# Moving TensorE's transposes and attention products one to three k tiles later in its order

## The chip, the cores and the metric

The kernel runs on one core of a Trainium2 chip. The metric is the device time of one execution in microseconds (us); lower is better. Three runs of the kernel before took 2409.83, 2411.72 and 2412.51 us (median 2411.72). For this kernel a difference of about 0.2% (4.8 us) is what can be told from no change.

## The reference

Two transformer-like blocks in float32 over 256 tokens of width 2048. The first block mixes a gated causal convolution with a causal attention that adds a forgetting bias, then a square-ReLU feed-forward of width 8192. The second block has attention with a relative-position bias, a multi-window pooling branch, and a gated feed-forward of width 5632 whose up-projection passes a three-tap causal convolution. Cut to what the change touches:

```
q, k = heads; p = softmax(q @ k.T * scale + bias); a = p @ v          # both blocks, 8 heads
u = rmsnorm(x) @ w_up                                                  # 2048 -> 2 * 5632
y = conv_b + conv_w[0]*u[t-2] + conv_w[1]*u[t-1] + conv_w[2]*u[t]
gate, val = split(y);  x = x + (silu(gate) * val) @ w_down
```

## The kernel before

Every large product is cut into chunks of up to 512 output columns (`add_chunk`). A chunk reads weight tiles of 512 rows; a weight tile is four k tiles of 128 rows, and two k tiles make a unit. Each weight is split on chip into a high part `wh` (a cast on ScalarE, L846) and a remainder `wl` (a subtraction on VectorE, L847); the activations are split likewise into two halves of a `k_...` tile (`split_out`, L155 to L166). One k tile costs TensorE six matmuls (`both`, L887): high by high, low by high and high by low, for two token blocks. At the start of a unit the split of the unit three places ahead is issued (L901), and `wh` and `wl` have four buffers each, so ScalarE and VectorE run at most a few units ahead of TensorE.

TensorE's program order is written out by the kernel itself. The main loop (L898) issues a k tile, adds one to `now`, and then `run_due` takes up to three of the tasks from a heap whose due time has come. `later(delay, fn)` puts a task `delay` k tiles ahead, `chain` puts a row of steps at one k tile each, and `need(key)` runs tasks ahead of their due time until a named operand has been issued. The queues themselves run in the order of issue, so a task due at k tile 2 stands on TensorE behind two k tiles of the next chunk, and what comes after it waits with it.

At the end of a chunk its evacuation is issued: on ScalarE for the scaled chunks (`evac_scaled`, L440), on VectorE for the residual sum (`evac_add`, L543). The result must then be turned so that tokens lie along the free dimension. `turned` does that on VectorE in 16 small pieces; `transposed` does it on TensorE, as two tasks (b = 0 and 1) of four 128x128 transposes each (L175), `gap` k tiles apart, and chains the steps of its user behind each.

- In the up-projection of the second block, chunks alternate: a gate chunk "g" (turned on VectorE, then convolution L479 and L484, sigmoid L745, product L746) and a value chunk "v" (transposed on TensorE, then convolution, product with the gate L740, and the split into `k_d`, L155 and L162). There are 11 pairs, in groups of 4, 4 and 3; each group is followed by its down-projection, whose k tiles read `k_d` in the order of the pairs. The variable `soon` marks the very last v chunk (j = 10).
- When a chunk of the residual is finished, `to_acts` makes the next layer's activations from it. For the last of four (n == 3) TensorE transposes `xs[3]`; this happens for the layers named "f", "i" and "g" (and "h" at the start). `squares` (L227) and the norm's factor (`rstd_of`) follow at once; for "i" the tasks `final_norm` rescale `xs` later (L582).
- `head_task` issues the eight heads of either attention as seven tasks: scores, biased, exps, normal, turn (three transposes of the probabilities, L351), keep (a copy on ScalarE, L355) and values (L360, L361). Heads are 6 k tiles apart in the first block and 7 in the second. The second attention's last head feeds the output projection, which asks for it by `need("2a1 3")`.

Of the kernel before, what the change touches and what calls it, by code (L numbers as in the profile page):

```python
# [61 lines left out]
def tile_two_blocks(  # L62
# [30 lines left out]
    def later(delay, fn, *keys):  # L93
        seq[0] += 1
        heapq.heappush(tasks, (now[0] + delay, seq[0], fn, keys))

    def chain(delay, stages, *keys, gap=1):

        for i, fn in enumerate(stages):
            later(delay + i * gap, fn, *(keys if i == len(stages) - 1 else ()))  # L100
# [11 lines left out]
    def need(*keys):  # L112
        for key in keys:
            while key not in ready:
                run_one()


    xs = [const.tile([P, TB, CW], F32, name=f"x{n}") for n in range(4)]
# [28 lines left out]
    def split_out(key, j, n, p, scales=None):  # L147

        if key not in K:
            kt_tile(key)  # L150
        hi, lo = (K[key][:, h, j:j + n, :] for h in range(2))

        def to_hi():
            if scales is None:
                S.copy(hi, p)  # L155
            else:
                for i in range(n):
                    S.activation(hi[:, i, :], p[:, i, :], AF.Copy, scale=scales[i])

        def to_lo():  # L160
            if scales is None:
                V.tensor_tensor(out=lo, in0=p, in1=hi.bitcast(F32), op=OP.subtract)  # L162
            else:
                for i in range(n):
                    V.scalar_tensor_tensor(out=lo[:, i, :], in0=p[:, i, :], scalar=scales[i],
                                           in1=hi[:, i, :].bitcast(F32), op0=OP.mult, op1=OP.subtract)  # L166
        return [to_hi, to_lo]

    def transposed(z, use, delay, keys=(), gap=1, lag=1, step=1):

        def task(b, mine):
            p = tr_p.tile([P, 2, T], F32, tag="tr", name="p_t")
            for j in range(2):
                for tb in range(TB):
                    TE.transpose(p[:, j, tb * P:(tb + 1) * P], z[:, tb, (2 * b + j) * P:(2 * b + j + 1) * P], ident)  # L175
            chain(lag, use(b, p), *mine, gap=step)
        for b in range(2):
            later(delay + gap * b, lambda b=b: task(b, keys[2 * b:2 * b + 2]))
# [22 lines left out]
    def group_keys(key):  # L201
        return [f"{key} {j}" for j in range(4)]
# [38 lines left out]
    def to_acts(name, n, gcol, delay):  # L241

        key = f"{name}{n}"
        def use(b, p):
            return split_out(key, 2 * b, 2, p, [gcol[:, 4 * n + 2 * b + i:4 * n + 2 * b + i + 1] for i in range(2)])
        if name == "h" or n == 3:
            transposed(xs[n], use, delay, group_keys(key), lag=0, step=0)
        else:
            turned(xs[n], use, delay, group_keys(key), rate=2, lag=3)

# [54 lines left out]
    def head_task(blk, h, delay):  # L305

        half, hh = divmod(h, 4)
        cols = (slice(0, P), slice(P, MAXCOL))
        t = {}

        def scores():
            need(f"{blk}q{half} {hh}", f"{blk}k{half} {hh}")
            qk = AT[blk, "qk", half]
            p = t["p"] = tr_p.tile([P, 512], F32, tag="tr", name="p_s")
            TE.matmul(p[:, 0:P], qk[:, 0, hh, 0:P], qk[:, 1, hh, 0:P], start=True, stop=True)
            TE.matmul(p[:, P:3 * P], qk[:, 0, hh, P:T], qk[:, 1, hh, :], start=True, stop=True)  # L316

        def biased():
            if blk == 1:
                need(f"1nb{half}")  # L320
            nb, p = AT[blk, "nb", half], t["p"]
            s = t["s"] = s_p.tile([P, CW], F32, tag="s", name="s_att")[:, 0:MAXCOL]
            st = t["st"] = st_p.tile([P, 6], F32, tag="sm", name="sm")
            if blk == 1:
                for i in range(2):
                    V.scalar_tensor_tensor(out=s[:, cols[i]], in0=p[:, cols[i]], scalar=AT["c"][:, i, h:h + 1],
                                           in1=nb[:, hh, cols[i]], op0=OP.add, op1=OP.add)
            else:
                need(f"rq{half}")
                for i in range(2):  # L330
                    V.scalar_tensor_tensor(out=s[:, cols[i]], in0=p[:, cols[i]],
                                           scalar=AT["rq", half][:, 4 * i + hh:4 * i + hh + 1],
                                           in1=nb[:, hh, cols[i]], op0=OP.mult, op1=OP.add)
            for i in range(2):
                V.tensor_reduce(st[:, i:i + 1], s[:, cols[i]], AX.X, OP.max, negate=True)

        def exps():
            s, st = t["s"], t["st"]
            for i in range(2):
                S.activation(s[:, cols[i]], s[:, cols[i]], AF.Exp, bias=st[:, i:i + 1], accum_out=st[:, 2 + i:3 + i])  # L340

        def normal():
            s, st = t["s"], t["st"]
            V.reciprocal(st[:, 4:6], st[:, 2:4])
            for i in range(2):
                V.tensor_scalar(s[:, cols[i]], s[:, cols[i]], st[:, 4 + i:5 + i], None, op0=OP.mult)

        def turn():
            p = t["p"] = tr_p.tile([P, 512], F32, tag="tr", name="p_p")
            for i in range(3):  # L350
                TE.transpose(p[:, i * P:(i + 1) * P], t["s"][:, i * P:(i + 1) * P], ident)  # L351

        def keep():
            t["pt"] = pt_p.tile([P, MAXCOL], F32, tag="pt", name="pt")
            S.copy(t["pt"], t["p"][:, 0:MAXCOL])  # L355

        def values():
            v, pt = AT[blk, "v"], t["pt"]
            p = tr_p.tile([P, 2, T], F32, tag="tr", name="p_t")
            TE.matmul(p[:, 0, :], v[:, 0, h * P:(h + 1) * P], pt[:, 0:T], start=True, stop=False)  # L360
            TE.matmul(p[:, 0, P:T], v[:, 1, h * P:(h + 1) * P], pt[:, T:MAXCOL], start=False, stop=True)  # L361
            chain(1, split_out(f"{blk}a{half}", hh, 1, p[:, 0:1, :]), f"{blk}a{half} {hh}")
        for i, fn in zip((0, 1, 2, 3, 6, 7, 8), (scores, biased, exps, normal, turn, keep, values)):
            later(delay + i, fn)

    def qk_use(blk, half, which, scale=None):
# [108 lines left out]
    def conv3(o, u, w, bias):  # L475

        def last():
            for i in range(2):
                S.activation(o[:, i, :], u[:, i, :], AF.Identity, bias=bias(i), scale=w(i, 2))  # L479

        def before():
            for i in range(2):
                for d in (1, 2):
                    V.scalar_tensor_tensor(out=o[:, i, d:T], in0=u[:, i, 0:T - d], scalar=w(i, 2 - d), in1=o[:, i, d:T],  # L484
                                           op0=OP.mult, op1=OP.add)
        return [last, before]
# [242 lines left out]
    def evac_up(which, j, key):  # L729
        def then(z):  # L730
            cv = z_p.tile([P, 4, T], F32, tag="z", name="z_cv")

            def use(b, p):
                a = cv[:, 2 * b:2 * b + 2, :]
                c0 = (0 if which == "g" else 44) + 4 * j + 2 * b
                steps = conv3(a, p, lambda i, t: ccol[:, t, c0 + i:c0 + i + 1], lambda i: ccol[:, 3, c0 + i:c0 + i + 1])
                if which == "v":
                    g = FU["g", j][:, 2 * b:2 * b + 2, :]
                    need(f"gate{j} {2 * b}")
                    return steps + [lambda: V.tensor_tensor(out=a, in0=a, in1=g, op=OP.mult), *split_out(key, 2 * b, 2, a)]  # L740
                t = {}

                def sigmoid():
                    t["s"] = s_p.tile([P, 2, T], F32, tag="s", name="sg")
                    S.activation(t["s"], a, AF.Sigmoid)  # L745
                return steps + [sigmoid, lambda: V.tensor_tensor(out=a, in0=a, in1=t["s"], op=OP.mult)]  # L746
            if which == "g":
                FU["g", j] = cv
            if which == "g":
                turned(z, use, 2, group_keys(f"gate{j}"), rate=2)  # L750
            else:
                soon = j == FF2 // CW - 1
                transposed(z, use, 1 if soon else 2, group_keys(key), gap=1 if soon else 2)
        return then


# [204 lines left out]
```

## Time and profile before

| | us |
|---|---|
| median of three runs | 2411.72 |
| the profiled execution, own time | 2411.87 |
| its span, first to last instruction | 2410.1 |
| VectorE busy | 1662.6 (69%) |
| ScalarE busy | 1158.9 (48%) |

The profile is of one execution. "Idle before, releaser" in a row says how long the engine stood idle just before the instruction and what ended that. A busy matmul row is not a matmul at its peak, since matmuls are pipelined. The granted clock is 1.00 in nearly all of the 40 slices of the page; the mean of the execution is 0.995. Weights come by 1 MB transfers, 445.8 MB in all, at 189 GB/s over the span.

### The profile page before, as it was taken

Reading aid. Unit: us, or ns where it says so; the run is one execution under the profiler, and the core shown is the slowest. Engines: PE = TensorE matmul, PEld = TensorE weight load, DVE = VectorE, ACT = ScalarE, POOL = GpSimd, SP = SyncE. Lnnn points to the kernel's source line nnn. Section 1 sums busy time; section 2 is a strip of 40 time slices with the busy share of each in tenths; the row PEclk is TensorE's granted clock in tenths of the full one; section 3 lists DMA queues with packets and bytes.
Section 4 is the critical chain, followed back from the end, with each engine's and each line's share of the span. In section 5 each row is a group of like instructions: output and inputs, shape, how many; then the busy total and the mean of one; then the engine's idle time right before and its main releaser. Section 6 shows DMA issues by size and latency. Waiting matters only on the chain.

```text
span 2410.1 us, 27828 instructions
## 1 busy us (share of the span) xinstructions
PE 2369.9 (98%) x10649; PEld 1962.8 (81%) x10649; DVE 1662.6 (69%) x2293; ACT 1158.9 (48%) x1514; POOL 36.5 (2%) x53
## 2 busy tenths in 40 slices
PE   9899999999999999999999999999999999999999
PEld 9688888888888888888888887888778888888877
DVE  5487776666877567577477856667787467865884
ACT  5355444444454354354345446545555345544453
POOL 1000000000000000000000000000000000000000
PEclk9899999999999999999999999999999999999999
DMA  7755565655556556555555665555555555555554
GB/s 256 188 183 171 197 207 194 210 202 176 192 179 206 192 190 195 192 192 192 192 186 181 197 209 194 161 177 190 180 181 193 192 185 182 188 194 185 185 175 140
DMA packets 230966, 456.67 MB, mean 189 GB/s; under 512 B 8085, under 2 KB 15997, under 8 KB 230832
## 3 DMA queue, kind: packets, MB, share of 16 engines
q1 hardware_dynamic: 227584, 445.81, 56.4%
q0 software_dynamic: 3248, 9.08, 1.6%
q8 instruction: 83, 1.36, 0.2%
q14 instruction: 51, 0.42, 0.0%
HBM read 451.18 MB, written 3.67 MB: 189 GB/s over the span
## 4 chain that ended last, share of the span: by engine, by line
PE 88%; DVE 6%; ACT 3%; DMA 2%; issue 1%; SPq 0%; ACTq 0%
PE acc L887 85%; DVE wl L847 2%; DVE z_t L190 2%; ACT wh L846 2%; DMA raw<-in_w_in_dram 2%; DVE z_cv L484 1%; PE p_t L175 1%; ACT z L440 1%; PE acc_last L887 0%; ACT z_cv L479 0%; PE p_t L360 0%; PE p_s L316 0%; PE p_t L714 0%; PE p_p L351 0%; DVE x L543 0%
## 5 line engine op out<-in xcount | busy, mean ns | idle before, releaser
L847 DVE TENSOR_TENSOR wl<-raw,wh 128x1024 fp32r<-128x1024 f32 (+1 forms) x848 | 1022.1, 1214 | 653.1 <-ACT wh L846 565.2
L846 ACT CAST wh<-raw 128x1024 fp32r<-128x1024 f32 (+1 forms) x848 | 874.9, 1042 | 726.3 <-PE acc L887 671.0
L887 PE MATMUL acc<-wh,k_g 128*128 128x512 f32 x1408 | 379.3, 391 | 0.0
L887 PE MATMUL acc<-wh,k_h 128*128 128x512 f32 (+1 forms) x1344 | 352.5, 384 | 12.7 <-ACT wh L846 12.7
L887 PEld LDWEIGHTS acc<-wh,k_g 128*128 128x128 f32 x1408 | 263.6, 188 | 53.9
L887 PEld LDWEIGHTS acc<-wh,k_h 128*128 128x128 f32 x1344 | 248.5, 189 | 58.5 <-ACT wh L846 14.0
L887 PE MATMUL acc<-wh,k_u 128*128 128x512 f32 x1024 | 274.8, 389 | 4.5 <-DVE k_u L162 4.5
L887 PE MATMUL acc<-wh,k_f 128*128 128x512 f32 x1024 | 273.9, 389 | 0.0
L887 PEld LDWEIGHTS acc<-wh,k_u 128*128 128x128 f32 x1024 | 191.9, 188 | 45.8 <-DVE k_u L162 6.2
L887 PEld LDWEIGHTS acc<-wh,k_f 128*128 128x128 f32 x1024 | 192.1, 188 | 39.7
L887 PE MATMUL acc<-wl,k_g 128*128 128x512 f32 x704 | 217.5, 390 | 0.0
L887 PE MATMUL acc<-wl,k_h 128*128 128x512 f32 (+1 forms) x672 | 201.4, 381 | 0.0
L887 PE MATMUL acc<-wh,k_d 128*128 128x512 f32 x656 | 176.9, 392 | 0.0
L887 PE MATMUL acc<-wl,k_f 128*128 128x512 f32 x512 | 157.6, 389 | 0.0
L887 PE MATMUL acc<-wl,k_u 128*128 128x512 f32 x512 | 157.6, 389 | 0.0
L887 PEld LDWEIGHTS acc<-wl,k_g 128*128 128x128 f32 x704 | 132.6, 188 | 27.9
L190 DVE STREAM_TRANSPOSE z_t<-z 32x256 f32<-32x256 f32 x336 | 146.4, 436 | 5.6
L887 PEld LDWEIGHTS acc<-wl,k_h 128*128 128x128 f32 x672 | 125.4, 189 | 23.2 <-DVE wl L847 0.3
L887 PEld LDWEIGHTS acc<-wh,k_d 128*128 128x128 f32 x656 | 123.2, 189 | 25.2
L887 PE MATMUL acc<-wh,k_i 128*128 128x512 f32 x512 | 140.0, 395 | 0.0
L190 DVE STREAM_TRANSPOSE z_t<-z_f 32x256 f32<-32x256 f32 x256 | 111.5, 436 | 4.1
L887 PEld LDWEIGHTS acc<-wl,k_f 128*128 128x128 f32 x512 | 96.1, 188 | 20.0
(227 smaller groups left out, 2010.3 us busy)
## 6 DMA issues: line engine op xcount, KB each, us to landing
raw<-in_w_ff_dram SPq DMA_DIRECT2D x128, 1024.0 KB, 5.2
raw<-in_w_in_dram SPq DMA_DIRECT2D x104, 1024.0 KB, 5.1
raw<-in_w_up_dram SPq DMA_DIRECT2D x88, 1024.0 KB, 5.0
raw<-in_w_down_dram SPq DMA_DIRECT2D x44, 1024.0 KB, 5.1
raw<-in_w_mix_out_dram SPq DMA_DIRECT2D x16, 1024.0 KB, 5.1
raw<-in_w_out_dram SPq DMA_DIRECT2D x16, 1024.0 KB, 5.1
raw<-in_w_conv_out_dram SPq DMA_DIRECT2D x8, 1024.0 KB, 5.3
raw<-in_w_attn_out_dram SPq DMA_DIRECT2D x8, 1024.0 KB, 5.5
```

The lines of the kernel that those rows point to most:

```text
L175: TE.transpose(p[:, j, tb * P:(tb + 1) * P], z[:, tb, (2 * b + j) * P:(2 * b + j + 1) * P], ident)
L190: V.transpose(dst, src)
L440: S.activation(z[:, tb, :], acc[:, tb, :], AF.Copy, scale=R[rname][:, tb:tb + 1])
L484: V.scalar_tensor_tensor(out=o[:, i, d:T], in0=u[:, i, 0:T - d], scalar=w(i, 2 - d), in1=o[:, i, d:T], op0=OP.mult, op1=OP.add)
L846: S.copy(wh[:, :, 0:ncol], raw)
L847: V.tensor_tensor(out=wl[:, :, 0:ncol], in0=raw, in1=wh[:, :, 0:ncol].bitcast(F32), op=OP.subtract)
L887: TE.matmul(halves[tb][:, 0:ncol], k[:, i, kt, tb * P:(tb + 1) * P], w[:, kk, 0:ncol], start=begin and first and kt == 0, stop=end and stop)
```

## The change

Three places get other due times; no instruction is added or removed.

- `to_acts`: the transposes of the last residual chunk of the layers "f", "i" and "g" are due 5 and 6 k tiles after the evacuation instead of 2 and 3 ("h" is as it was).
- `head_task`: turn is due 7 k tiles after the head's start instead of 6, keep 8 instead of 7, values 10 instead of 8; the two split steps behind values move with it, from 9 and 10 to 11 and 12.
- `evac_up`, v chunks: the transposes are due at 3 and 5 instead of 2 and 4, and for the very last v chunk at 2 and 3 instead of 1 and 2; the five steps chained behind each move with them.

```diff
@@ to_acts
-            transposed(xs[n], use, delay, group_keys(key), lag=0, step=0)
+            transposed(xs[n], use, delay if name == "h" else delay + 3, group_keys(key), lag=0, step=0)
@@ head_task
-        for i, fn in zip((0, 1, 2, 3, 6, 7, 8), (scores, biased, exps, normal, turn, keep, values)):
+        for i, fn in zip((0, 1, 2, 3, 7, 8, 10), (scores, biased, exps, normal, turn, keep, values)):
@@ evac_up
-                transposed(z, use, 1 if soon else 2, group_keys(key), gap=1 if soon else 2)
+                transposed(z, use, 2 if soon else 3, group_keys(key), gap=1 if soon else 2)
```

## Rows read from the trace of the kernel before

**Rows 1.** Page, part 1: busy us of each engine (share of the span) xinstructions.

```profile
PE 2369.9 (98%) x10649; PEld 1962.8 (81%) x10649; DVE 1662.6 (69%) x2293; ACT 1158.9 (48%) x1514; POOL 36.5 (2%) x53
```

**Rows 2.** Waits of TensorE, whole span: us in total, times, longest us.

```profile
PE p_t L175 <- ACT z L440: 10.5, 22, 1.9
PE p_t L175 <- DVE x L543: 4.8, 3, 1.6
...
PE p_t L360 <- ACT pt L355: 1.4, 1, 1.4
...
PE p_p L351 <- DVE s_att L346: 0.6, 1, 0.6
PE acc L887 <- DVE k_2a L162: 0.5, 1, 0.5
```

**Rows 3.** Timeline at a v chunk's end: start us, us, engine, line, idle before.

```profile
1750.82 1.07 PE L887 MATMUL acc<-wh,k_g 128*128 128x512 f32 x4
...
1752.18 1.07 PE L887 MATMUL acc<-wh,k_g 128*128 128x512 f32 x4
...
1753.45 1.26 ACT L440 ACTIVATE z<-acc,r 128x512 f32<-128x512 f32 x2
1754.19 0.33 PE L175 MATMUL p_t<-cc,z 128*128 128x128 f32 x1 [0.49 <-ACT z L440]
...
1754.39 3.65 DVE L847 TENSOR_TENSOR wl<-raw,wh 128x1024 fp32r<-128x1024 f32 x3
...
1754.77 0.55 PE L175 MATMUL p_t<-cc,z 128*128 128x128 f32 x3 [0.25 <-ACT z L440]
...
1757.96 1.90 DVE L484 SCALAR_TENSOR_TENSOR z_cv<-p_t,ccol,z_cv 128x255 f32<-128x255 f32 x4
```

**Rows 4.** Timeline at the first v chunk's end.

```profile
1706.25 1.25 ACT L440 ACTIVATE z<-acc,r 128x512 f32<-128x512 f32 x2
1706.98 0.33 PE L175 MATMUL p_t<-cc,z 128*128 128x128 f32 x1 [1.42 <-ACT z L440]
```

**Rows 5.** Windows: length, busy PE, PEld, DVE, ACT, POOL; granted clock; DMA, GB/s.

```profile
1708.00:1713.00 5.00, 5.00 (x19) 3.97 (x19) 4.75 (x8) 3.45 (x6) 0.00 (x0) 0.66 0.90 314
2340.00:2345.00 5.00, 5.00 (x20) 4.04 (x19) 3.40 (x5) 3.66 (x6) 0.00 (x0) 0.66 0.85 281
660.00:665.00 5.00, 3.41 (x19) 2.93 (x20) 2.55 (x9) 3.44 (x8) 0.72 (x1) 1.00 0.41 152
```

**Rows 6.** Timeline at the last v chunk's end.

```profile
2338.48 1.26 ACT L440 ACTIVATE z<-acc,r 128x512 f32<-128x512 f32 x2
...
2339.21 0.33 PE L175 MATMUL p_t<-cc,z 128*128 128x128 f32 x1 [1.85 <-ACT z L440]
...
2340.56 1.03 ACT L479 ACTIVATE z_cv<-p_t,ccol 128x256 f32<-128x256 f32 x2
2340.70 1.23 DVE L847 TENSOR_TENSOR wl<-raw,wh 128x1024 fp32r<-128x1024 f32 x1 [0.32 <-ACT wh L846]
...
2350.41 0.69 DVE L162 TENSOR_TENSOR k_d<-z_cv,k_d 128x512 fp32r<-128x512 f32 x1
...
2351.81 1.07 PE L887 MATMUL acc<-wh,k_d 128*128 128x512 f32 x4
```

**Rows 7.** Timeline at the layer "f": the residual's last chunk.

```profile
660.32 1.22 DVE L543 TENSOR_TENSOR x<-x,acc 128x1024 f32<-128x1024 f32 x1
...
661.59 0.66 PE L175 MATMUL p_t<-cc,x 128*128 128x128 f32 x4 [1.63 <-DVE x L543]
...
662.81 1.03 ACT L846 CAST wh<-raw 128x1024 fp32r<-128x1024 f32 x1
```

**Rows 8.** Timeline at the layer "i", behind the second rescaling.

```profile
1380.91 2.93 ACT L846 CAST wh<-raw 128x1024 fp32r<-128x1024 f32 x3
...
1383.63 1.07 PE L887 MATMUL acc<-wh,k_i 128*128 128x512 f32 x4
```

**Rows 9.** Timeline in the up-projection, soon after a gate chunk's end.

```profile
1731.49 1.23 DVE L847 TENSOR_TENSOR wl<-raw,wh 128x1024 fp32r<-128x1024 f32 x1 [3.05 <-PE acc L887]
```

## The prediction

> **What bounds the kernel now.** I read the busy times first: TensorE is busy for 2369.9 of the span's 2410.1 us [rows 1]. Only the other 40.2 us, and what the clock loses beside them, can be won by a change of order. Which waits these are stands in TensorE's list of waits [rows 2]. Four of its entries are of instructions that the change moves: the transposes L175 behind ScalarE's evacuation (10.5 us in 22 waits) and behind the residual sum (4.8 us in 3), the attention's values behind the copy of the probabilities (1.4 us) and its turn behind the normalisation (0.6 us). The wait for `k_2a` stands in the same list and is not of a moved instruction. So at most 10.5 + 4.8 + 1.4 + 0.6 = 17.3 us of waiting can go. The timeline then shows where the next k tile is at hand while TensorE waits, and the windows show the clock.
>
> A k tile is the unit of every shift: two starts of its four high-part matmuls stand at 1750.82 and 1752.18, so it lasts 1.36 us [rows 3].
>
> **The change part by part.** No instruction comes or goes: 8 transposes in each of 11 v chunks, 8 in each of three layers, and the three transposes, one copy and four products of each of 16 heads change places with k tiles that TensorE would do anyway. Each moved step drags its chain along, on ScalarE and VectorE, past the split of the next unit. The move is worth the wait that it covers, less what the chain then makes late. No DMA is issued by a moved step, so SP's and POOL's queues keep their order.
>
> *Nine ordinary v chunks.* The evacuation runs from 1753.45 to 1754.71, two activations behind the gate chunk's sigmoids, and TensorE waits 0.49 us for its first half and 0.25 us for its second [rows 3]. In the 22 waits the first and last v chunk take 1.42 + 0.25 and 1.85 + 0.25 (the 0.25 is there as in [rows 3]; the first numbers are in [rows 4, 6]), so the other nine hold 10.5 - 1.67 - 2.10 = 6.7 us, 0.75 each. One k tile of 1.36 us now stands ahead of the transposes: without waiting they would come at 1753.70 + 1.36 = 1755.06, after 1754.71, 0.35 us to spare. The k tile taken forward belongs to the next unit, whose casts stand ahead of the evacuation on ScalarE, so its weights are there. Gain 6.7 us. What the evacuation itself waits for is not moved earlier or later against the gate chunk's end: VectorE stands idle 3.05 us soon after that end [rows 9], so each pair starts with no backlog.
>
> The chain behind is late by more than the shift: the convolution's VectorE half (four operations, 1.90 us, 1757.96 [rows 3]) falls behind the next unit's remainder. In an ordinary pair nobody needs `k_d` before the down-projection, and the two groups of four need it 12 and 14 k tiles after the chunk's end, some 16 and 19 us, while the last step is due at 10. I carry no cost there.
>
> *The first v chunk.* The evacuation ends at 1706.25 + 1.25 = 1707.50 and TensorE had stopped at 1706.98 - 1.42 = 1705.56 [rows 4]. One k tile reaches 1706.92, so 0.06 + 0.25 = 0.31 us stay of 1.67. Gain 1.36 us. Right behind the old wait the granted clock was 0.66 over 5 us, partly at the lower level of 1.2 GHz, which costs 5 x 0.34 = 1.7 us [rows 5]. With a wait of 0.31 I take this as gone, since 0.49 + 0.25 at the nine others leaves it at 1.00 on the page. Together 3.1 us; without the clock 1.4.
>
> *The last v chunk.* Here the operand is needed at once: the down-projection's third tile reads it, at its k tile 8. Before, TensorE waited until 2339.21, then lost 1.7 us to the clock [rows 5], and asked for the low half of `k_d` about 0.45 us after 2351.81; that half was finished at 2350.41 + 0.69 = 2351.10 [rows 6]. So 1.16 us were to spare. Now one k tile goes ahead and the wait shrinks from 2.10 to 0.74, but the chain still starts when the evacuation ends, 2339.74. I follow VectorE's queue in the new order from 1.23 us behind 2340.70 [rows 6]: another remainder to 2343.1; the convolution, which waits for a cast and for ScalarE's two convolution rows of 1.03, to 2345.0; a remainder to 2346.2; the product 0.69 to 2346.9; the second half's convolution 1.90 to 2348.8 and product to 2349.5; a remainder to 2350.7; the low half to 2351.4. TensorE, at full clock, would ask for it at 2349.6. It waits 1.85 us there, and passes 2351.4 instead of 2352.26: gain 0.8 us of the 3.8 that stood there (2.10 + 1.7). Both ends: 3.5 if the chain is not late, and 0.8 - 1.7 = -0.9 if the new wait brings the lower clock again. Waits of 1.42 and 1.85 us were followed by it, one of 1.63 was not [rows 4 to 7], so I take 0.8, where the queue puts it. The Trainium skill (TensorE: Matmul & The Clock Gate, section "A second HAM failure mode: psum-queue depth-cycling") says that frequent short idle times between groups of matmuls let the clock fall and rise, and that the price is paid between the bursts. By that rule the new wait would be priced like the old one, the term here would be -0.9 and the total 14.1 us; the trace agrees at two of its fourteen such places.
>
> *Layers "f", "i", "g".* The sum ends at 660.32 + 1.22 = 661.54 and TensorE waits 1.63 us for it [rows 7]; the other two hold (4.8 - 1.63)/2 = 1.58 each. Three k tiles are 4.1 us, so the waits go. The operand is needed at the twelfth k tile, six behind the new transposes. What is late next is the split of the fourth unit, queued on ScalarE behind the squares of the same sum; it ends at 662.81 + 1.03 = 663.84 [rows 7], and TensorE asks for it near 666.3, six k tiles after the chunk's start. Gain at "f" and "g": 3.2 us. At "i" VectorE and ScalarE also rescale and square `xs`: ScalarE comes to the cast of the chunk's last unit at 1380.91 [rows 8], its first cast ends 0.98 later (2.93/3), and TensorE came for it at 1383.63, 1.7 us on. Now TensorE comes 1.58 us earlier plus what the transposes shift, near 1381.7, and the two `k_i` steps, 0.8 us each on ScalarE, now stand behind the first rescaling. I get the cast at 1382.5 and the remainder 0.35 us late: 1.25 of 1.58 come back as a wait, gain 0.3 (bounds 1.6 and -0.5).
>
> *Attention.* Turn moves by one k tile, more than the 0.6 us of its wait; values move by two, keep by one, so the copy gets one k tile more, against a wait of 1.4 us [rows 2]. Up to 2.0 us can go; the copy now stands behind one more ScalarE step and I take 1.7 (bounds 0 and 2.0). At the end `need` asks for the last head's result two k tiles before its new due time, so values, high and low half are issued back to back there: the wait of 0.5 us for `k_2a` [rows 2] stays about as it is, since then as now a remainder on VectorE ends just ahead of the low half.
>
> *Sum.* 6.7 + 3.1 + 0.8 + 3.5 + 1.7 = 15.8 us. The profiled execution took 2411.87 us, 1.8 more than its span and 0.15 more than the median: 2411.87 - 15.8 = 2396.1, and against the median 2395.9. I predict **2396.0 us**.
>
> **The rivals.**
>
> *All is covered.* Nothing comes back at "i", at the last chunk or in attention: 10.5 - 0.3 + 2 x 1.7 + 4.8 + 2.0 = 20.4, so 2391.4 us. For it: VectorE is busy for only 69% [rows 1]. Against it: the queue that I followed at the last chunk.
>
> *The wait comes back later.* TensorE's lead is 0.75 us per pair; if the evacuation's time hangs on a ScalarE and VectorE that never catch up, the nine ordinary waits and the smaller gains return: 15.8 - 6.7 - 0.8 - 0.3 = 8.0, so 2403.9 us. For it: the evacuation already starts 2.6 us behind the next chunk's first k tile (1753.45 against 1750.82 [rows 3]). Against it: VectorE's 3.05 us of idleness [rows 9].
>
> *Slower.* In each v chunk's second half both convolutions (2 x 1.90 us, [rows 3]) now stand behind a remainder and ahead of the next; if the units behind them have no store of weights, TensorE waits 3.8 - 1.36 = 2.44 us per chunk for `wl`: 11 x 2.44 = 26.8, less 15.8, so 2422.9 us. It decides from 15.8/11 = 1.44 us per chunk on. Against it: VectorE works off three remainders from 1754.39 on, before the convolution [rows 3].
>
> *It does not do what it says.* The three-task limit or `need` puts the steps where they were, or each wait moves to the next instruction in turn: 2411.7 us. Against it: in the v chunks two tasks are due at a time, and only one `need` bites.
>
> **How the numbers follow.** Forecast 0.60, all covered 0.12, comes back later 0.17, slower 0.05, without effect 0.06. The range for 8 in 10 runs from 2391.0, just below "all is covered", to 2404.0, where the waits return; the forecast's own bounds (last chunk -0.9 to 3.5, "i" -0.5 to 1.6, attention 0 to 2.0, clock 1.4 or 3.1) give 2391.8 to 2402.0. A difference of 0.2%, 4.8 us, is about what can be told from none: faster beyond that 0.89, within it 0.06, slower 0.05.
>
> **What would show it.** After, TensorE's list of waits should have no L175 behind L440 beyond 0.3 us at the first v chunk and 0.74 at the last, no L175 behind L543, and a new wait of L887 for `k_d` of about 1.9 us near the end, and for a cast of about 1 us in the chunk behind layer "i". The clock should stay at 1.00 near the first v chunk. The prediction is wrong if ordinary v chunks still show waits at L175, if L887 waits for `wl` in them, or if TensorE's idle time falls by 13 us and the time does not follow.

## The result, and the profile after

The changed kernel took 2394.19 us (median of 5 runs, 2393.11 to 2395.26), the kernel before 2410.56 us beside it (median of 5, 2409.83 to 2412.51): a ratio of 0.9930, 95% interval 0.9920 to 0.9941, or 16.4 us less. The profiled execution took 2393.52 us (span 2391.8, mean granted clock 0.997), 18.35 us less than the profiled execution of before. The two differences disagree by 2.0 us because before's profiled execution lay 1.3 us above its median and after's 0.7 below; what follows is read from the two profiles, and the times of the experiments are set against it.

The busy times of the engines (us, share of the span, instructions) answer to [rows 1]:

```profile
PE 2362.4 (99%) x10649; PEld 1960.1 (82%) x10649; DVE 1662.8 (70%) x2293; ACT 1159.0 (48%) x1514; POOL 36.7 (2%) x53
```

TensorE executes the same 10649 matmuls, and its busy time fell by 7.5 us; its idle time, span less busy, fell by 10.8, from 40.2 to 29.4. So two fifths of the gain were never in the idle column, on which all the prediction's terms but the clock's rest. Two parts of these 7.5 us are to be seen below: four transposes broken by a wait count 0.33 + 0.55 us, unbroken 0.60; and of the stretches at the lower clock behind the waits of this change two went and one came.

TensorE's list of waits, whole span (us in total, times, longest us), answers to [rows 2]:

```profile
PE acc L887 <- ACT wh L846: 12.9, 3, 11.1
PE acc L887 <- DVE k_u L162: 4.5, 4, 1.1
PE p_t L360 <- ACT pt L355: 1.9, 1, 1.9
PE acc L887 <- DVE k_d L162: 1.5, 1, 1.5
...
PE p_t L175 <- ACT z L440: 1.0, 3, 0.5
...
PE acc L887 <- ACT k_2a L155: 0.5, 1, 0.5
```

The 22 waits behind L440 are 3, of 1.0 us instead of 10.5; the three behind the residual sum L543 are gone; so is the one of L351. Two came at the places of the change: for `k_d` (1.5 us) and, as the third of the waits for `wh`, one of 0.65 us. One grew: L360 behind the copy L355, 1.4 to 1.9 us. The wait for `k_2a` kept its size, but it is for the high half from ScalarE (L155) now and was for the low half from VectorE (L162). Small waits near the kernel's start, of instructions that the change doesn't move, differ too.

The timeline of after at the first v chunk's end, an ordinary one and the last one (start us, us, engine, line, idle before) answers to [rows 4, 3, 6]:

```profile
1703.24 0.33 PE L175 MATMUL p_t<-cc,z 128*128 128x128 f32 x1
...
1703.81 0.55 PE L175 MATMUL p_t<-cc,z 128*128 128x128 f32 x3 [0.24 <-ACT z L440]
...
1746.84 1.26 ACT L440 ACTIVATE z<-acc,r 128x512 f32<-128x512 f32 x2
1748.26 0.60 PE L175 MATMUL p_t<-cc,z 128*128 128x128 f32 x4
...
1748.62 1.17 PE L887 MATMUL acc<-wh,k_g 128*128 128x512 f32 x4
...
2322.01 0.33 PE L175 MATMUL p_t<-cc,z 128*128 128x128 f32 x1 [0.50 <-ACT z L440]
...
2322.59 0.55 PE L175 MATMUL p_t<-cc,z 128*128 128x128 f32 x3 [0.25 <-ACT z L440]
...
2331.63 0.61 PE L887 MATMUL acc<-wh,k_d 128*128 128x512 f32 x2
...
2333.76 0.73 PE L887 MATMUL acc<-wh,k_d 128*128 128x512 f32 x2 [1.52 <-DVE k_d L162]
```

In the ordinary chunk the evacuation ends at 1748.10 and the transposes start at 1748.26 as one row of four: no wait, and nothing split. At the first chunk only the second half waits, 0.24 us. At the last, 0.75 us stay and 1.52 us are added at the down-projection.

Windows of after behind these places and behind attention's wait (length, busy PE, PEld, DVE, ACT, POOL; granted clock; DMA, GB/s) answer to [rows 5]:

```profile
1495.00:1500.00 5.00, 4.87 (x16) 3.92 (x16) 3.33 (x7) 3.22 (x8) 0.00 (x0) 0.66 0.65 210
1705.00:1710.00 5.00, 5.00 (x26) 4.09 (x25) 4.52 (x6) 4.49 (x7) 0.00 (x0) 1.00 0.96 329
2323.00:2328.00 5.00, 5.00 (x26) 4.13 (x25) 4.60 (x8) 4.20 (x7) 0.00 (x0) 1.00 0.90 298
2333.00:2338.00 5.00, 4.24 (x19) 3.50 (x20) 3.44 (x5) 1.69 (x2) 0.00 (x0) 1.00 0.07 23
```

The clock now stays at 1.00 behind the first and the last v chunk, and also behind the new wait for `k_d`. In attention it fell to 0.66 over 5 us; before, it had not fallen there:

```profile
1495.00:1500.00 5.00, 4.50 (x21) 3.79 (x22) 2.98 (x6) 2.86 (x8) 0.00 (x0) 1.00 0.61 201
```

Each trace is one execution. Whether the clock falls behind one and the same wait differs between executions, as the experiments and the last section show, so what the table below gains or loses by the clock holds for these two executions only.

**Where the time came from.** The same instruction is looked up in both traces, and its start of after is taken from its start of before; the difference between two such places is what the stretch between them gained.

| from ... to | before, after (start us) | lead | gain of the stretch | forecast |
|---|---|---|---|---|
| start ... layer "f" | 656.62, 656.43 | 0.19 | 0.2 | 0 |
| ... chunk behind "i" (residual "f") | 1361.86, 1359.94 | 1.92 | 1.73 | 1.6 |
| ... its 15th k tile ("i") | 1384.99, 1382.55 | 2.44 | 0.52 | 0.3 |
| ... first gate chunk (second attention) | 1656.43, 1654.47 | 1.96 | -0.48 | 1.7 (both attentions) |
| ... end of the first chunk pair ("g" and the first v chunk) | 1715.46, 1708.80 | 6.66 | 1.79 + 2.91 | 1.6 + 3.1 |
| ... last group's down-projection (nine ordinary) | 2335.84, 2318.64 | 17.20 | 10.54 | 6.7 |
| ... behind the last v chunk's `k_d` | 2353.17, 2334.80 | 18.37 | 1.17 | 0.8 |

The sum was 15.8 and is 18.4 in these two traces; by the medians it is 16.4. Two terms are off: the nine ordinary v chunks gave 3.8 us more, attention 2.2 us less.

### The profile page after: what moved, and what is told of

Its sections match the earlier page's. It is cut to its first block, busy times and chain, and to the rows that moved or that the text cites. A ratio compares the mean times of both kernels' runs of the same rounds, so it can differ in the third digit from the quotient of the medians.

```text
span 2391.8 us, 27807 instructions
## 1 busy us (share of the span) xinstructions
PE 2362.4 (99%) x10649; PEld 1960.1 (82%) x10649; DVE 1662.8 (70%) x2293; ACT 1159.0 (48%) x1514; POOL 36.7 (2%) x53
## 3 DMA queue, kind: packets, MB, share of 16 engines
q8 instruction: 83, 1.36, 0.2%
## 4 chain that ended last, share of the span: by engine, by line
PE 91%; DVE 4%; DMA 2%; ACT 1%; issue 1%; SPq 0%; POOL 0%; ACTq 0%; DVEq 0%
PE acc L887 89%; DMA raw<-in_w_in_dram 2%; DVE wl L847 2%; DVE z_t L190 1%; ACT wh L846 1%; PE p_t L175 1%; PE acc_last L887 0%; DVE z_cv L484 0%; PE p_t L360 0%; PE p_s L316 0%; PE p_t L714 0%; DVE k_i L165 0%; PE p_p L351 0%; ACT junk L227 0%; DMA bg<-in_g_final_dram 0%
## 5 line engine op out<-in xcount | busy, mean ns | idle before, releaser
L887 PEld LDWEIGHTS acc<-wl,k_u 128*128 128x128 f32 x512 | 96.1, 188 | 20.0
```

The costliest lines, as they stand in the source:

```text
L887: TE.matmul(halves[tb][:, 0:ncol], k[:, i, kt, tb * P:(tb + 1) * P], w[:, kk, 0:ncol], start=begin and first and kt == 0, stop=end and stop)
```

## The experiments

Each edit stands against the kernel named with it; times are medians, the ratio is to the kernel before on the same chip, with its 95% interval. Theory 1 takes the prices from the table above; theory 2 takes those of the prediction, or puts the gain elsewhere.

**Only the v chunks.** Against before:

```diff
-                transposed(z, use, 1 if soon else 2, group_keys(key), gap=1 if soon else 2)
+                transposed(z, use, 2 if soon else 3, group_keys(key), gap=1 if soon else 2)
```

> Only the v chunks' transposes are moved (3 and 5, the last 2 and 3); layers f, i, g and the heads are as before. Theory 1, that a wait costs TensorE the stretch between the k tiles on either side of it (2.89 us against 1.73 with no wait, so 1.16 per ordinary v chunk): 9 x 1.16 = 10.4, plus 2.9 at the first and 1.2 at the last v chunk, 14.5 us less, near 2396. Theory 2, that it costs the idle column alone (0.75 per chunk): 6.7 + 3.1 + 0.8 = 10.6 us less, near 2400, and the rest of the gain of the whole change must then show in the other two parts. In the trace theory 1 expects each pair of chunks to repeat every 44.5 us, theory 2 every 44.9; before it was 45.7.

2397.17 against 2411.43 us, ratio 0.9944 [0.9929, 0.9958]: 14.3 us, theory 1's number. The chain of waits of this kernel, from 1740 to 1850 us (start us, us, what), has the stretch between the two halves of the transposes at

```profile
1753.81 2.76 PE acc L887 x12
...
1798.29 2.76 PE acc L887 x12
```

so a pair of chunks takes 44.48 us (1798.29 - 1753.81). Before, it takes 45.68 us: the evacuation L440 of a v chunk stands at 1753.45 [rows 3], and two pairs on, in the timeline of before, at

```profile
1844.81 1.25 ACT L440 ACTIVATE z<-acc,r 128x512 f32<-128x512 f32 x2
```

The difference is 1.2 us per pair, where the prediction had 0.75.

**Only the layers.** Against before:

```diff
-            transposed(xs[n], use, delay, group_keys(key), lag=0, step=0)
+            transposed(xs[n], use, delay if name == "h" else delay + 3, group_keys(key), lag=0, step=0)
```

> Only the transposes of layers f, i and g are moved by three k tiles. The ledger of the two traces says 1.7 + 0.5 + 1.8 = 4.0 us less, near 2406.6, with a wait for a cast of about 0.6 us behind layer i. Its rival, that TensorE's lead there is taken back by the next wait for k_u or by the up-projection's evacuations: no gain, 2410.6.

2406.74 against 2411.43 us, ratio 0.9983 [0.9973, 0.9993]: 4.7 us. No wait behind L543 is left, and the third wait for `wh` is there. The table's three layer terms make 1.73 + 0.52 + 1.79 = 4.0.

**Only attention.** Against before:

```diff
-        for i, fn in zip((0, 1, 2, 3, 6, 7, 8), (scores, biased, exps, normal, turn, keep, values)):
+        for i, fn in zip((0, 1, 2, 3, 7, 8, 10), (scores, biased, exps, normal, turn, keep, values)):
```

> Only the heads' turn, keep and values are moved. The prediction on record: 1.7 us less, near 2408.9. The ledger of the two traces: half a microsecond more, near 2411.1, since the copy of the probabilities in the second attention now stands behind two more steps on ScalarE, TensorE waits 1.9 us for it instead of 1.4, and the clock falls to its lower level behind that wait, 1.7 us. If the clock does not fall here, 1.2 us less, near 2409.4.

2411.28 against 2411.43 us, ratio 0.9998 [0.9989, 1.0008]: no effect that can be told. A gain of 1.7 us would be 0.9993, inside that interval, so it is the trace that decides. Timeline, then window, of this kernel:

```profile
1498.62 0.70 PE L360 MATMUL p_t<-pt,k_v 128*128 128x256 f32 x2 [1.88 <-ACT pt L355]
...
1499.30 1.91 PE L887 MATMUL acc<-wh,k_i 128*128 128x512 f32 x4
```

```profile
1498.00:1503.00 5.00, 4.38 (x13) 3.57 (x14) 3.11 (x6) 3.23 (x9) 0.00 (x0) 0.66 0.65 210
```

The wait grew from 1.36 to 1.88 us and the next four matmuls took 1.91 us instead of 1.18, at a clock of 0.66: this edit brings the longer wait by itself, and in this execution the lower clock behind it. TensorE's lead over before falls by 0.48 us between the places of the table's third and fourth row, as in the whole change.

The same trace shows what the clock alone is worth at the two v chunks that this kernel leaves as they were. They waited as before, but the clock stayed at 1.00 behind both. Timeline, then windows, of this kernel:

```profile
1708.52 0.33 PE L175 MATMUL p_t<-cc,z 128*128 128x128 f32 x1 [1.41 <-ACT z L440]
...
2339.27 0.33 PE L175 MATMUL p_t<-cc,z 128*128 128x128 f32 x1 [1.84 <-ACT z L440]
```

```profile
1709.00:1714.00 5.00, 4.91 (x25) 4.13 (x26) 4.93 (x7) 4.81 (x8) 0.00 (x0) 1.00 0.86 287
2340.00:2345.00 5.00, 5.00 (x26) 4.20 (x26) 4.02 (x6) 3.96 (x7) 0.00 (x0) 1.00 0.86 290
```

With nothing moved there, this kernel gains 1.55 us on before over the stretch with the first v chunk (1656.43 to 1715.46 before, 1657.98 to 1715.46 here) and 1.59 us over the one with the last (2335.84 to 2353.17 before, 2335.90 to 2351.63 here).

**All but attention.** Against the changed kernel:

```diff
-        for i, fn in zip((0, 1, 2, 3, 7, 8, 10), (scores, biased, exps, normal, turn, keep, values)):
+        for i, fn in zip((0, 1, 2, 3, 6, 7, 8), (scores, biased, exps, normal, turn, keep, values)):
```

> The whole change without the heads' part. By the prediction on record it loses 1.7 us against the whole change, 2395.9. By the ledger it gains half a microsecond, 2393.7, and the late copy shows a wait of 1.4 us at full clock. A difference this small is read from the trace: TensorE's lead over the kernel before at the start of the up-projection, 1.96 us with the whole change, should be near 2.5.

2393.00 against 2411.43 us, ratio 0.9925 [0.9911, 0.9940], no slower than the whole change. Its lead over before is 2.66 us at the table's third place and 2.71 at the fourth: with attention as before, nothing is won or lost there. ScalarE's timeline shows what the moved attention does. This kernel, in which attention keeps its old due times:

```profile
1483.74 2.23 ACT L846 CAST wh<-raw 128x1024 fp32r<-128x1024 f32 x2
1491.69 0.72 ACT L373 ACTIVATE k_qk<-z_t,vcol 128x512 f32<-128x512 f32 x1 [5.71 <-DVE z_t L190]
1492.31 0.46 ACT L355 COPY pt<-p_p 128x384 f32<-128x384 f32 x1
1492.67 0.72 ACT L373 ACTIVATE k_qk<-z_t,vcol 128x512 f32<-128x512 f32 x1
1493.30 1.04 ACT L846 CAST wh<-raw 128x1024 fp32r<-128x1024 f32 x1
```

Its TensorE:

```profile
1492.83 0.70 PE L360 MATMUL p_t<-pt,k_v 128*128 128x256 f32 x2 [1.37 <-ACT pt L355]
```

The changed kernel, ScalarE and then TensorE:

```profile
1483.73 1.04 ACT L846 CAST wh<-raw 128x1024 fp32r<-128x1024 f32 x1
...
1491.48 0.73 ACT L373 ACTIVATE k_qk<-z_t,vcol 128x512 f32<-128x512 f32 x1 [6.44 <-DVE z_t L190]
...
1492.11 1.04 ACT L846 CAST wh<-raw 128x1024 fp32r<-128x1024 f32 x1
...
1493.06 0.71 ACT L373 ACTIVATE k_qk<-z_t,vcol 128x512 f32<-128x512 f32 x1
...
1493.68 1.03 ACT L846 CAST wh<-raw 128x1024 fp32r<-128x1024 f32 x1
...
1494.61 0.47 ACT L355 COPY pt<-p_p 128x384 f32<-128x384 f32 x1
...
1495.13 0.70 PE L360 MATMUL p_t<-pt,k_v 128*128 128x256 f32 x2 [1.90 <-ACT pt L355]
...
1495.81 1.79 PE L887 MATMUL acc<-wh,k_i 128*128 128x512 f32 x4
```

Read the bracket of the first L373 and then the place of L355. ScalarE had stood 5.71 to 6.44 us waiting for VectorE to turn a chunk, and comes free only now. Counted from that L373, with the old due times the copy stands second in its queue; issued one k tile later it stands fifth, behind two casts and a further L373. One cast and the further L373 got in front by the later place of the copy. The other cast got there another way: with the old due times two casts were done ahead of the first L373 (1483.74, x2), now only one is, and the second has to wait behind it. Counted in time from the first L373's start, the copy now ends 1495.08 - 1491.48 = 3.60 us on instead of 1492.77 - 1491.69 = 1.08, so 2.5 us later. TensorE comes for it 1495.13 - 1.90 - 1491.48 = 1.75 us on instead of 0.23 us ahead (its row stands at 1492.83, after a wait of 1.37), so only 2.0 us later: two k tiles of 1.36, less what the turn no longer waits. The wait is longer by the difference, 0.5 us.

**One k tile more ahead of the v transposes.** Against the changed kernel:

```diff
-                transposed(z, use, 2 if soon else 3, group_keys(key), gap=1 if soon else 2)
+                transposed(z, use, 2 if soon else 4, group_keys(key), gap=1 if soon else 2)
```

> The whole change, with the v chunks' transposes (but the last's) one k tile later still, at 4 and 6. Theory 1: one k tile covered all but the 0.2 us at the first v chunk, so nothing more is to be won: 2394.0, pairs of chunks again every 44.5 us, no wait for k_d but the one near the end. Its rival, that the gain grows with the distance because ScalarE's evacuation is what paces a pair: 44.1 us or less per pair, near 2390.

2393.26 against 2410.72 us, ratio 0.9928 [0.9913, 0.9943]. The pair is 44.48 us again, and only the last chunk's 0.7 us behind L440 is left: nothing more to win there.

**The last v chunk as before.** Against the changed kernel:

```diff
-                transposed(z, use, 2 if soon else 3, group_keys(key), gap=1 if soon else 2)
+                transposed(z, use, 1 if soon else 3, group_keys(key), gap=1 if soon else 2)
```

> The whole change, but the very last v chunk's transposes at 1 and 2 as in the kernel before. Theory: the end of the chunk goes back to a wait of 2.1 us, half the clock for some 3.4 us behind it (1.7 us), and no wait for k_d: 1.2 us more than the whole change, 2395.4. If the clock does not fall this time, the shorter of the two: 0.5 us less than the whole change.

2396.17 against 2410.72 us, ratio 0.9935 [0.9919, 0.9952]. Timeline and window of this kernel:

```profile
2323.66 0.33 PE L175 MATMUL p_t<-cc,z 128*128 128x128 f32 x1 [1.87 <-ACT z L440]
```

```profile
2323.00:2328.00 5.00, 4.09 (x15) 3.21 (x16) 3.10 (x5) 4.19 (x7) 0.00 (x0) 0.66 0.69 215
```

The old wait and, in this execution, the lower clock behind it are back, and the wait for `k_d` is gone: the one comes where the other goes, as the prediction's queue had it. Over the stretch with the last v chunk the lead grows by 0.07 us, where the whole change has 1.17.

Attention is moved in this kernel as in the whole change, and TensorE's wait for the copy is as long, but the clock did not fall behind it. Timeline and window of this kernel:

```profile
1498.36 0.70 PE L360 MATMUL p_t<-pt,k_v 128*128 128x256 f32 x2 [1.87 <-ACT pt L355]
```

```profile
1499.00:1504.00 5.00, 5.00 (x25) 4.16 (x24) 3.29 (x10) 3.73 (x8) 0.00 (x0) 1.00 0.59 197
```

Between the table's third and fourth place this kernel gains 1.07 us on before (1384.99 to 1656.43 before, 1385.76 to 1656.12 here), where the whole change, with the lower clock, loses 0.48.

**Only the first half of the v transposes later.** Against the changed kernel:

```diff
-                transposed(z, use, 2 if soon else 3, group_keys(key), gap=1 if soon else 2)
+                transposed(z, use, 2 if soon else 3, group_keys(key), gap=1)
```

> The whole change, but only the first half of each v chunk's transposes is moved (3 instead of 2); the second half stays at 4, so its chain is not moved. Only the first half ever waited. Theory 1, the wait and the four transposes that could not overlap their neighbours, lies in the first half alone: 44.5 us per pair, 2394.2, as the whole change. Its rival, that the 0.4 us per pair beyond the idle column come from the chain behind the second half standing later: 44.9 us per pair, near 2398.

2394.58 against 2410.72 us, ratio 0.9931 [0.9916, 0.9946]; a pair takes 44.46 us. The second half is where it was before the change, and the gain is whole: it lies in the first half's wait.

**Values later still.** Against the changed kernel:

```diff
-        for i, fn in zip((0, 1, 2, 3, 7, 8, 10), (scores, biased, exps, normal, turn, keep, values)):
+        for i, fn in zip((0, 1, 2, 3, 7, 8, 12), (scores, biased, exps, normal, turn, keep, values)):
```

> The whole change with the heads' values at 12 instead of 10. Theory: the copy of the probabilities is late by ScalarE's queue (two copies of k_qk that wait for VectorE's turned pieces, and two casts), not by its own place; two k tiles more, 2.7 us, cover the 1.9 us wait, and the lower clock behind it goes too: 1.9 + 1.7 less, some 3.5 us, near 2390.7. Its rival, that the wait only moves on to the next operand there (scores, or a cast): within 1 us of 2394.2.

2392.41 against 2410.72 us, ratio 0.9922 [0.9907, 0.9937]. The wait for the copy is gone and the clock stays at 1.00, but the next operand is late in its place:

```profile
1501.68 0.61 PE L351 MATMUL p_p<-cc,s_att 128*128 128x128 f32 x3 [1.58 <-DVE s_att L346]
```

It is 1.8 us faster than the changed kernel, half of what theory 1 expected and more than its rival did. Such differences are smaller than what can be told between kernels here; the trace has attention gain 0.82 us on before (lead 1.73, then 2.55).

**Turn and keep later too.** Against the changed kernel:

```diff
-        for i, fn in zip((0, 1, 2, 3, 7, 8, 10), (scores, biased, exps, normal, turn, keep, values)):
+        for i, fn in zip((0, 1, 2, 3, 8, 9, 12), (scores, biased, exps, normal, turn, keep, values)):
```

> The whole change with the heads' turn at 8, keep at 9 and values at 12. With values alone at 12, the copy's wait went and a new one of 1.6 us came at the next head's turn, since TensorE now got there before VectorE had normalised. Theory: both steps need the distance; turn one k tile later still takes 1.4 of these 1.6 us away, and nothing else in the second attention is late by more than 0.5 us: 1.4 us less than with values alone at 12, near 2391.0. Its rival, that VectorE and ScalarE are the bound through the second attention, so that each cover moves the wait to a later instruction: 2392.4 again.

2394.95 against 2410.03 us, ratio 0.9934 [0.9921, 0.9948]. The expectation (near 2391.0) was missed. The rival's mechanism came true, not its number (2392.4): L351 no longer waits, and some 14 us on the transposes of the following chunk do. A wait of 0.6 us for the copy is back too.

```profile
1515.95 0.63 PE L175 MATMUL p_t<-cc,z 128*128 128x128 f32 x4 [2.75 <-DVE z L619]
```

Over the 5 us behind it the granted clock was 0.66 again, so this kernel gives back more than the one above had won. In attention it loses 1.37 us on before. With values later the wait went from the copy (ScalarE) to `s_att` (VectorE), with turn later too to `z` (VectorE): in this stretch each cover moved the wait to the next operand that these two make, and the last is the longest.

**The second rescaling later.** Against the kernel just shown:

```diff
-                later(3 + 5 * m, lambda m=m: final_norm(m))
+                later(7 + 4 * m, lambda m=m: final_norm(m))
```

> As the run with turn at 8 and values at 12, and at layer i the four rescalings of xs are due at 7, 11, 15 and 19 k tiles instead of 3, 8, 13 and 18, behind the last activation tile's steps instead of ahead of them. Theory: the 0.6 us wait for a cast behind layer i comes from ScalarE's squares of the rescaled xs standing in front of that cast; with the order exchanged it goes, 0.8 us less than the run beside it. Its rival, that the later rescalings make r3 late for the values of the second attention: a wait of some microseconds for the evacuation of the first chunk of v, more than the run beside it.

2394.87 against 2410.03 us, ratio 0.9935 [0.9922, 0.9947]. The wait for the cast behind "i" is gone (two waits for `wh` instead of three), so the rescaling's place ahead of that cast was its cause. In the time it can't be seen. In the trace it is worth more than the 0.6 us of the idle column: at "i", between the table's second and third place, the lead over before grows by 1.80 us, about as at "f" and "g", where the whole change has 0.52.

**The two that helped, together; and the rescaling without attention.** Against the changed kernel:

```diff
-        for i, fn in zip((0, 1, 2, 3, 7, 8, 10), (scores, biased, exps, normal, turn, keep, values)):
+        for i, fn in zip((0, 1, 2, 3, 7, 8, 12), (scores, biased, exps, normal, turn, keep, values)):
...
-                later(3 + 5 * m, lambda m=m: final_norm(m))
+                later(7 + 4 * m, lambda m=m: final_norm(m))
```

> The whole change with the heads' values at 12 (turn 7, keep 8) and the rescalings at layer i due at 7, 11, 15 and 19. By the traces the two gains stand in different stretches and add up: 1.8 us for the values, 0.7 us for the wait behind layer i, 2391.7 against 2394.2 for the whole change. Its rival: the lead won at layer i is used up by the second attention's next late operand, 2392.4.

2390.87 us (2390.09 to 2391.70) against 2409.82, ratio 0.9920 [0.9907, 0.9934]: the lowest time of all, 18.9 us below its kernel before where the change has 16.4. Its runs don't overlap the changed kernel's, but the two intervals do. The same rescaling with attention at its old due times:

```diff
-        for i, fn in zip((0, 1, 2, 3, 7, 8, 10), (scores, biased, exps, normal, turn, keep, values)):
+        for i, fn in zip((0, 1, 2, 3, 6, 7, 8), (scores, biased, exps, normal, turn, keep, values)):
...
-                later(3 + 5 * m, lambda m=m: final_norm(m))
+                later(7 + 4 * m, lambda m=m: final_norm(m))
```

> The whole change without the heads' part, with the rescalings at layer i due at 7, 11, 15 and 19. Theory: 0.7 us less than without the heads' part alone, 2392.3, waits of 0.6 and 1.4 us in the second attention as in the kernel before. Its rival, that TensorE's lead there makes these two waits longer by what was won: 2393.0.

2391.84 us against 2409.82, ratio 0.9924 [0.9912, 0.9937]. The window over the chunk behind "i" of the first of the two has TensorE busy without a gap:

```profile
1350.00:1400.00 50.00, 50.00 (x226) 41.42 (x225) 38.90 (x60) 28.58 (x48) 3.56 (x6) 1.00 0.68 213
```

The 1.0 us between the two is within what their runs scatter, so which due times are best in attention stays open.

## Why the prediction was right, and which terms were not

The likeliest case came: the time follows TensorE's idle time, and 2394.2 stands for 2396.0. The bounds that the forecast gave itself held for the whole; not for two terms, whose errors have opposite signs. That they nearly cancel is luck.

**The nine ordinary v chunks: right mechanism, price too low (6.7, measured 10.5).** The prediction took the idle column, 0.49 + 0.25 us, as the price of the wait [rows 3]. The price is larger, and the trace of before has it. The same four transposes appear there once with the wait and once, in the chunk's second half, without; the k tiles around them, on TensorE:

```profile
1755.07 1.18 PE L887 MATMUL acc<-wh,k_g 128*128 128x512 f32 x4
...
1756.54 1.07 PE L887 MATMUL acc<-wh,k_g 128*128 128x512 f32 x4
...
1757.91 0.60 PE L175 MATMUL p_t<-cc,z 128*128 128x128 f32 x4
1758.27 1.17 PE L887 MATMUL acc<-wh,k_g 128*128 128x512 f32 x4
```

Without a wait, from one k tile's start to the next across the transposes is 1758.27 - 1756.54 = 1.73 us. With it, from 1752.18 [rows 3] to 1755.07, it is 2.89. The wait costs 1.16 us, not 0.74. Unwaited, the four transposes take 0.60 us as a row but add only 1.73 - 1.36 = 0.37, because they overlap the matmuls on both sides; a wait in front of them and one in the middle take that overlap away, and no column of the row says so. Nine times 1.16 is 10.4, the table has 10.54, and the experiments with the v chunks alone (1.2 per pair) and with the first half alone agree. Because the price sat in the first half's break, a later second half adds nothing.

**The first v chunk: right, with a clock term that not every execution pays.** 2.91 of 3.1. The wait is 0.24 (0.31 forecast) and the clock stays at 1.00. But the kernel with attention alone, in which this chunk is not moved, gained 1.55 us there because the clock stayed up behind the old wait. What is left for the move, 1.36 us, is the forecast's term without the clock. The prediction took the lower clock of one execution as what the old wait always costs. Its ground for 1.00 behind short waits, the page, has the clock in tenths only (9 for 90% or more); nine windows of 5 us behind the ordinary chunks of before confirm it, 1.00 each.

**The last v chunk: right for these two executions.** 1.17 for 0.8. The wait behind L440 is 0.75 (0.74 forecast) and that for `k_d` 1.52 (1.85 forecast). The clock stayed at 1.00 behind both. By the rule on frequent short idle times (the Trainium skill, TensorE: Matmul & The Clock Gate, section "A second HAM failure mode: psum-queue depth-cycling") this term would have been -0.9; this trace does not show it there. Here too the gain rests on the clock behind the old wait: the kernel with attention alone, with that wait and the clock at 1.00, gained 1.59 us where the moved chunk has 1.17. By these figures, moving this chunk wins nothing in an execution whose clock does not fall behind the old wait.

**The layers: right.** "f" and "g" gave 1.73 + 1.79 = 3.52 for 3.2. At "i" the forecast had a new wait of 1.25 us for the cast behind the rescaled squares; it came, 0.65 us long, and the gain is 0.52 for 0.3:

```profile
1378.35 0.64 ACT L227 ACTIVATE junk<-x 128x512 f32<-128x512 f32 x1 [2.32 <-DVE x L582]
...
1379.64 2.93 ACT L846 CAST wh<-raw 128x1024 fp32r<-128x1024 f32 x3
...
1380.72 1.21 PE L887 MATMUL acc<-wh,k_i 128*128 128x512 f32 x4 [0.65 <-ACT wh L846]
```

That is the timeline of after: the cast starts when the squares are through, and TensorE comes for it before it ends. Moving the rescaling took this wait away.

**Attention: wrong (1.7, measured -0.5).** The step that failed is "the copy gets one k tile more". It holds for TensorE's order; the copy's own queue was treated as one step longer. In fact, at the one head where ScalarE had a backlog, two casts and one L373 stand between the first L373 and the copy that did not before, and the copy came later by more than the k tile given. So a wait that was to go grew, from 1.36 to 1.90 us. The bound of 0 failed by a second thing that the term left out: behind this wait the clock fell in the profiled execution, 5 x 0.34 = 1.7 us in the window shown. It need not fall: with the same attention and a wait of 1.87 us the kernel with the last v chunk as before kept 1.00 and gained 1.07 us on this stretch. So the longer wait is shown to be the change's doing; that the term came out below 0 is the clock of this execution.

The lead over before shows where the rest lies. It is 2.44 us at the table's third place, 2.63 ahead of the late copy's head (1486.51 before), 3.21 just behind it, ahead of the lower clock (1499.01), 1.51 when the clock is up again (1501.73), 1.86 behind the next head (1511.96), and 1.86 to 1.96 from there on. Without the clock that is a gain of 1.2 us, although the copy's wait lost 0.54. Turn and its neighbours must therefore have won some 1.7 us, not the 0.6 of its idle column. No run isolates this; it is the same sign of error as at the v chunks. It comes from the first three heads: the later ones gain nothing. The first attention has none of these waits, and a head there lasts as long as before (9.87 us, before 9.88).

**`k_2a`: right in size, not in its reason.** 0.46 us as before. The prediction had it stay because a remainder on VectorE would again end just ahead of the low half; now it is ScalarE's high half (L155) that TensorE waits for.

**The rivals.** "All is covered" (2391.4) fails at three places: `k_d`, the cast behind "i", and attention. "The wait comes back later" (2403.9) is excluded in the v chunks, where a pair lasts 44.5 us throughout. "Slower" needed waits for `wl` in the v chunks, and there are none in the list. "Without effect" fell with the interval.

## What to carry to other kernels

Read the price of a wait in front of small matmuls from the starts of the large ones around it, against the same place without a wait: the idle column alone was a third too low here. When a step is moved in a written-out order, look at each in-order queue on which it lands and count what now stands ahead of it, at the place where that queue has a backlog: one k tile of delay, with a cast that changed places, cost the copy 2.5 us. A stretch at the lower clock in one trace is not yet the price of the wait ahead of it: look for the same wait in other executions before the clock enters a sum. Where other engines pace a stretch, covering one operand only moves the wait to the next, so test each cover by itself.

## What the runs showed of the hardware

The same wait of TensorE was followed by the lower clock in some executions and not in others. The table takes the waits spoken of above in all fourteen traces (before, after and the twelve experiments). "Fell" means a granted clock of 0.66 or 0.67 over 5 us behind the wait, a mean of the two levels 1.2 and 2.4 GHz; otherwise it was 1.00.

| wait | length (us) | fell in | stayed at 1.00 in |
|---|---|---|---|
| copy of the probabilities, old due times | 1.36 to 1.37 | none | 5 (before among them) |
| first v chunk, not moved | 1.41 to 1.42 | before, layers alone | attention alone |
| new wait for `k_d` | 1.50 to 1.56 | none | 10 (after among them) |
| `s_att`, values at 12 | 1.56 to 1.58 | none | 2 |
| residual sum at "f", "i", "g" | 1.58 to 1.63 | none | 9 (three places in before, v alone, attention alone) |
| last v chunk, not moved | 1.84 to 1.87 | before, layers alone, last as before | attention alone |
| copy, moved by one k tile | 1.87 to 1.90 | after, attention alone, v one more, first half only | last as before |
| `z` behind turn at 8 | 2.75 to 2.76 | 2 of 2 | none |

Of the waits of 1.84 us or more 9 of 11 brought the lower clock, of those of 1.50 to 1.63 none of 21, and yet 2 of 3 of those of 1.41 to 1.42 did. Length alone does not order them, and no run shows what else does. Such a wait has to be priced with and without some 1.7 us. The executions of one kernel differ accordingly: those of before that were timed with the first four experiments have granted clocks from 0.994 (2414.69 us) to 0.997 (2408.74 us).
